# A hybrid retention / state-space block: matmuls of the state-space parts tied behind the projections and spread over v, phase powers and uT laid out contiguously, the query decay moved into the group norm

## The chip, the core and the metric

The kernel runs on one core of a Trainium2 chip. The metric is the time of one execution on the device in microseconds; lower is better. Three runs of the kernel before are shown, and one further execution, the profiled one, left the trace that every row below comes from.

## What is computed

One decoder block in float32: x has 1024 positions of 1024 channels. `w_in` gives q, k, v, gate (512 channels each) and u (512). Four retention heads of 128 work on q, k, v; 32 groups of 16 channels of u go through a diagonal state-space model with 64 complex states each; the two results go through `w_out`, and a squared-ReLU MLP with 4096 hidden channels follows. What matters here, cut from the reference:

```python
h = rmsnorm(x, norm_mix_pre[i]);  proj = h @ w_in[i]
q, k, v, gate, u = jnp.split(proj, [512, 1024, 1536, 2048], axis=-1)
...
s = jnp.einsum('bnihk,bnjhk->bnhij', q, k) * decay          # chunks of 128 positions
inner = jnp.einsum('bnhij,bnjhd->bnihd', s, v)
xi = jnp.exp((idx + 1.0)[None, :] * log_gamma[:, None])     # decay of a query's row
cross = jnp.einsum('bnihk,bnhkd,hi->bnihd', q, R_prev, xi)
y_ret = head_groupnorm(inner + cross)                       # (y - mean) * rsqrt(var + 1e-6) * g
...
states = associative_scan(a2 * a1, a2 * x1 + x2)            # over positions, complex
y_ssm = gelu(real(states @ c) + d_skip * u);  a, b = split(y_ssm @ w_glu[i])
x = x + rmsnorm(concat([y_ret, a * sigmoid(b)]) @ w_out[i], norm_mix_post[i])
m = square(relu(rmsnorm(x, norm_mlp_pre[i]) @ w_ff1[i])) @ w_ff2[i]
x = x + rmsnorm(m, norm_mlp_post[i])
```

## The kernel before

Large products keep float32 accuracy with three passes: ScalarE (ACT) rounds an operand to its high part `hi_*` (L135, L138), VectorE (DVE) subtracts to get the low part `lo_*` (L136), and `mm3` issues three matmuls of 128x512 (L106: hi·hi, hi·lo, lo·hi). Activations lie channels by positions, in two halves of 512 positions (`hf`), so most tiles are 128x512. A scheduler orders each engine's instructions when the program is built, and `tc.add_manual_dep` adds order where the code wants it: `mm` notes every large matmul in `marks`, `load` puts a DMA on SyncE's queue (SP, L115) not earlier than a mark some us back, and SP's queue issues in order, so a DMA that waits holds up those behind it.

The stages in time order, with the stretch each has in the profile:

- u projection (to 52 us): four tiles a half. ACT copies each from PSUM to `us` (L276) and the broadcast norm factor to `R` (L282). DVE multiplies them into `uT` (L285), writing 8 interleaved positions apart (`p t n`, with 64 x 8 read the other way), and SP writes uT to DRAM (`ud`), from where eight DMAs a part gather `UT` (positions by 8 times 16 channels on the partitions).
- small tables for the state-space model, on DVE, then the phase powers `fa` (16 powers) and `fb` (16 powers of the 16th), by repeated complex products on GpSimd (POOL, `double_up`, L312 to L317 with engine `GP`): one chain of 50 small instructions. A complex product takes six instructions (`cmul`).
- gate projections `pg` of the four heads, then q and k projections `pj` of heads 0 and 1, then `v_all`, then q and k of heads 2 and 3. Each half of a projection is 24 large matmuls, and so is each of v's 8 blocks. Between them the generator `side` runs the state-space parts in 24 steps: `tick()` advances it by one in each half of a gate, q or k projection, `v_all` in every second of its blocks. So 16 steps fall ahead of v, 4 into v, and 4 into the projections of heads 2 and 3.
- `ssm_part(ei)`, eight parts of four groups: `phase_tables` for every second part (L312 to L317 with engine `V`: `Fr`, `Fi` from `fa` and `fb`, 128x512), `W` and `VV` (outer products, three DVE instructions each, L493 to L495), `kps` (L502), `MR` (a memset by GpSimd at L506 and eight DMAs), `wps`, then `xps` (L522) from `UT`, the products with the phases on DVE (L523 to L526), the scan (L529), `SS` (L539), `MT` on ACT (L541), and `yps` (L544, L545), whose second matmul of each group needs `SS`. Gelu and a DMA to `yd` end a part.
- retention per head and half (`head_half`): `st`, masked by `dm`; `kz`, the states `Rs`; q is multiplied by `xis` (L630) and meets `Rs` in `y` (L638); group norm, and a transposition into the gate's tile.
- GLU (`gl`), W_out (`mx`), the norms, and the MLP from about 450 us to the end, which the change leaves as it is.

TensorE (PE) takes its instructions in order: a state-space matmul that is not ready holds up the projections behind it.

Of the kernel before, what the change touches and what calls it, by code (L numbers as in the profile page):

```python
# [18 lines left out]
AF = mybir.ActivationFunctionType  # L19
# [5 lines left out]
P = 128  # L25
# [3 lines left out]
T = 8  # L29
# [21 lines left out]
def hybrid_block_kernel(ctx, tc, x, xrow, gain, wu, wv, wqkg, wglu, wout, wff1, wff2, lam, bc, dsk,  # L51
# [116 lines left out]
    gains = const("gains", [P, 36])  # L168
    load(gains, gain)
    g_pre, g_post = gains[:, 0:8], gains[:, 8:16]  # L170
# [48 lines left out]
    def rstd(name, sums, n):  # L219
# [4 lines left out]
        return r  # L224

    def in_place(gen):

        n, last[0] = len(marks), None
        next(gen, None)
        stat[0] = last[0]  # L230
        if stat[0] is not None:
            tc.add_manual_dep(stat[0].ins, marks[n - 1][1].name, gate_info, reason="in order")
# [34 lines left out]
    for hf in range(2):  # L267
        n64 = slice(hf * 64, hf * 64 + 64)
        pss = [acc_ps(f"u_{hf}_{b}") for b in range(4)]
        for k in range(KB):  # L270
            for b in range(4):
                mm3(pss[b], tuple(z[:, b * P:(b + 1) * P] for z in wus[k]), hT[k][hf],
                    k == 0, k == KB - 1)
        us = [half(f"us_{hf}{b}") for b in range(4)]
        for b in range(4):
            S.activation(us[b], pss[b], AF.Copy)  # L276
        sums = xsum[:, 0, 4 * hf:4 * hf + 4]
        V.tensor_tensor(sums, sums, xsum[:, 1, 4 * hf:4 * hf + 4], op=ADD)
        rr = rstd(f"x{hf}", sums, 4)
        rv.append(rr)  # L280
        R.append(half(f"R{hf}"))
        S.activation(R[hf], norm_bcast(f"x{hf}", rr, 4), AF.Copy)  # L282
        for b in range(4):
            uT = half(f"uT_{hf}{b}", shape=(P, T, 64))
            V.tensor_tensor(uT.rearrange("p t n -> p n t"), us[b].rearrange("p (n t) -> p n t", t=T),  # L285
                            R[hf].rearrange("p (n t) -> p n t", t=T), op=MUL)
            load(ud[:, b * P:(b + 1) * P, n64].rearrange("t c n -> c t n"), uT)
# [123 lines left out]
    G2 = G // 2  # L411
    fa = half("fa", shape=(P, 2, 16, G2))
    fa_r, fa_i = fa[:, 0], fa[:, 1]
    fb = half("fb", shape=(P, 2, T, G))[:, :, :, 0:G2]
# [35 lines left out]
    def phase_tables(j):  # L450

        gs = slice(4 * j, 4 * j + 4)
        shf = [P, 4, T, 16]

        def lowp(m):
            return m[:, :, gs].rearrange("p a g -> p g a").unsqueeze(2).to_broadcast(shf)

        def highp(m):
            return m[:, :, gs].rearrange("p a g -> p g a").unsqueeze(3).to_broadcast(shf)

        def v4(m):
            return m.rearrange("p g (b a) -> p g b a", a=16)

        even, odd = ([half(f"F{z}{2 * j + i}", shape=s3) for z in "ri"] for i in range(2))
        tr, ti = half(f"ftr{j}", shape=s3), half(f"fti{j}", shape=s3)
        cmul(V, V, v4(even[0]), v4(even[1]), lowp(fa_r), lowp(fa_i), highp(fbr), highp(fbi),
             v4(tr), v4(ti))
        for e, o in zip(even, odd):
            load(o[0:64], e[64:128])
            load(o[64:128], e[64:128])  # L470
            load(e[64:128], e[0:64])
        phases[2 * j], phases[2 * j + 1] = even, odd

    def ssm_part(ei):
# [26 lines left out]
        for g in range(4):  # L501
            TE.matmul(kps[:, g], W[:, g], cs[:, g0 + g], start=True, stop=True)  # L502
        S.activation(kt, kps, AF.Copy)
# [17 lines left out]
        for g in range(4):  # L521
            TE.matmul(xps[:, g], WT[:, g], UT[:, g], start=True, stop=True)  # L522
        V.tensor_tensor(A, xps, Fr, op=MUL)  # L523
# [19 lines left out]
        for g in range(4):  # L543
            TE.matmul(yps[:, g], MT[:, g], UT[:, g], start=True, stop=False)  # L544
            TE.matmul(yps[:, g], VV[:, g], SS[:, g], start=False, stop=True)  # L545
# [15 lines left out]
    def step(n=1):  # L561
        for _ in range(n):
            next(side, None)
# [4 lines left out]
    def v_all():  # L568
# [3 lines left out]
        for c in range(NCH):  # L572
            if c % 2 == 0:
                step(1)
            ps = acc_ps(f"v_{c}")
# [8 lines left out]
    for i in range(2):  # L584
# [6 lines left out]
        tabs.append(pair)  # L591
    dm, xis = half("dm", shape=(P, H, P)), half("xis", shape=(P, H, P))
    load(dm, dmask, 10.0)
    load(xis, xi, 10.0)
    zet = const("zet", [P, H])
# [10 lines left out]
    def head_half(h, hh, qh, kh, sgt, Rs, gam):  # L606
# [16 lines left out]
        for i in range(n_s):  # L623
# [3 lines left out]
            else:  # L627
                V.scalar_tensor_tensor(Rs[c // 4][:, c % 4], Rs[(c - 1) // 4][:, (c - 1) % 4], gam,
                                       sps[:, i], op0=MUL, op1=ADD)
        V.tensor_tensor(q_, q_, xis[:, h].unsqueeze(1).to_broadcast(list(s3)), op=MUL)  # L630
        yield
# [10 lines left out]
        rs, nmr = ring("rs", (P, 4), 3), ring("nmr", (P, 4), 3)  # L642
        V.tensor_scalar(rs, mv[:, :, 1], EPS, None, op0=ADD)
        GP.tensor_tensor(rs, rs, mhalf[:, 0:4], op=ALU.pow)
# [527 lines left out]
def _constants():  # L1172
# [11 lines left out]
    dmask = np.where(diff[:, None, :] >= 0,  # L1184
                     np.exp(np.maximum(diff, 0.0)[:, None, :] * lg[None, :, None]), 0.0) * scale
    xi = np.broadcast_to(np.exp((loc + 1.0)[None, None, :] * lg[None, :, None]), (P, H, P))
    zeta = np.exp((P - 1 - loc)[:, None] * lg[None, :]) * scale
# [71 lines left out]
```

## Time and profile before

| quantity | value |
|---|---|
| runs | 1079.92, 1077.33, 1080.24 us (median 1079.92) |
| profiled execution, its own time | 1078.81 us |
| span of its trace | 1076.0 us |
| TensorE | 1048.2 us busy, 97% |
| VectorE / ScalarE / GpSimd | 72% / 46% / 7% busy |

The span is from the first to the last instruction; the 2.8 us beside it lie around the program. A row of a timeline has the start in us, the duration, engine, line, operation, output and inputs, shape, and, in brackets, how long the engine had been idle before it and what released it. PE's instructions overlap, so its rows last longer (0.39 us) than the distance of their starts (0.227 us for a 128x512 matmul); a lost time is read from the starts. A float32 matmul of a state-space part stands as two records.

### The profile page before, as it was taken

To read this page: it belongs to the slowest core of one execution; us is meant where nothing else is said; L and a number is where in the kernel's file an instruction comes from. 1 tells how busy PE (TensorE), PEld (TensorE's weight loads), DVE (VectorE), ACT (ScalarE), POOL (GpSimd) and SP (SyncE) were. 2 spreads that over 40 slices of the span, in tenths; PEclk is the share of its full clock that TensorE was granted. 3 is DMA by queue.
4 is the path that set the end of the run, shared out by engine and by line. 5 is a ranking of instruction groups with operands and counts; after the bars stand their busy time and mean duration, and the time that the engine had idled before them with its cause. 6 is when DMAs were issued, how large, how long until landed. Compare 5 with 4: busy or idle time off the path is not lost.

```text
span 1076.0 us, 14905 instructions
## 1 busy us (share of the span) xinstructions
PE 1048.2 (97%) x5056; PEld 879.4 (82%) x5056; DVE 769.5 (72%) x1446; ACT 490.9 (46%) x916; POOL 74.1 (7%) x101
## 2 busy tenths in 40 slices
PE   7999999999999999999999999999999999999995
PEld 6878778888888788788888888888888888888895
DVE  7979998278775207478888888877763885765965
ACT  7512343154564324466644444564731553524712
POOL 0360000000100222300000000000000000000002
PEclk9999999999999999999999999999999999999998
DMA  9735342042421105396366666656972665569424
GB/s 327 255 77 137 92 128 82 19 118 74 140 72 40 40 1 196 116 314 226 126 226 233 235 232 231 210 185 212 376 276 75 190 210 165 180 218 340 137 84 152
DMA packets 126283, 181.55 MB, mean 169 GB/s; under 512 B 35584, under 2 KB 43776, under 8 KB 126208
## 3 DMA queue, kind: packets, MB, share of 16 engines
q1 hardware_dynamic: 125664, 180.09, 50.5%
q8 instruction: 39, 0.64, 0.2%
q10 hardware_dynamic: 544, 0.52, 0.1%
q14 instruction: 36, 0.29, 0.1%
HBM read 130.62 MB, written 45.61 MB: 164 GB/s over the span
## 4 chain that ended last, share of the span: by engine, by line
PE 79%; DVE 6%; DMA 3%; POOL 2%; issue 2%; ACT 2%; SPq 1%; DVEq 0%; ACTq 0%; POOLq 0%
PE f2x L106 15%; PE f2y L106 12%; PE f1z L106 8%; PE f1y L106 8%; PE mx L106 8%; PE f1x L106 8%; PE pj L106 5%; PE v L106 4%; PE f1w L106 4%; PE gl L106 3%; SPq L115 1%; DMA yd<-Y 1%; PE sps L622 1%; DMA raw_wglu<-wglu_dram 1%; PE y L636 0%
## 5 line engine op out<-in xcount | busy, mean ns | idle before, releaser
L106 PE MATMUL f2x<-hi_tc,lo_sb 128*128 128x512 f32 x216 | 84.0, 389 | 0.0
L106 PE MATMUL f2x<-lo_tc,hi_sb 128*128 128x512 f32 x216 | 84.0, 389 | 0.0
L106 PE MATMUL f2x<-hi_tc,hi_sb 128*128 128x512 f32 x216 | 83.7, 390 | 0.0
L135 ACT ACTIVATE hi_sa<-rawa 128x512 fp32r<-128x512 f32 x80 | 48.4, 623 | 60.3 <-DVE rawa L828 57.1
L106 PE MATMUL f2y<-hi_tc,hi_sb 128*128 128x512 f32 x192 | 74.7, 389 | 0.0
L106 PE MATMUL f2y<-lo_tc,hi_sb 128*128 128x512 f32 x192 | 74.7, 389 | 0.0
L106 PE MATMUL f2y<-hi_tc,lo_sb 128*128 128x512 f32 x192 | 74.7, 389 | 0.0
L136 DVE TENSOR_TENSOR lo_sa<-rawa,hi_sa 128x512 fp32r<-128x512 f32 x80 | 56.5, 712 | 10.3 <-ACT hi_sa L135 10.3
L223 POOL TENSOR_TENSOR small<-small 128x4 f32<-128x4 f32 (+1 forms) x9 | 11.7, 1303 | 658.6 <-DVE small L221 628.1
L106 PE MATMUL pj<-hi_h,hi_wqkg 128*128 128x512 f32 x128 | 51.1, 399 | 0.0
L106 PE MATMUL pj<-hi_h,lo_wqkg 128*128 128x512 f32 x128 | 50.3, 393 | 0.0
L106 PE MATMUL pj<-lo_h,hi_wqkg 128*128 128x512 f32 x128 | 50.3, 393 | 0.0
L106 PE MATMUL f1x<-lo_tb,hi_sa 128*128 128x512 f32 x128 | 49.9, 390 | 0.3 <-DVE lo_tb L136 0.3
L106 PE MATMUL f1x<-hi_tb,hi_sa 128*128 128x512 f32 x128 | 50.1, 392 | 0.0
L106 PE MATMUL f1y<-hi_tb,hi_sa 128*128 128x512 f32 x128 | 49.8, 389 | 0.0
L106 PE MATMUL f1y<-lo_tb,hi_sa 128*128 128x512 f32 x128 | 49.8, 389 | 0.0
L106 PE MATMUL f1y<-hi_tb,lo_sa 128*128 128x512 f32 x128 | 49.8, 389 | 0.0
L106 PE MATMUL f1z<-hi_tb,hi_sa 128*128 128x512 f32 x128 | 49.8, 389 | 0.0
L106 PE MATMUL f1z<-lo_tb,hi_sa 128*128 128x512 f32 x128 | 49.8, 389 | 0.0
L106 PE MATMUL f1z<-hi_tb,lo_sa 128*128 128x512 f32 x128 | 49.8, 389 | 0.0
L106 PE MATMUL f1x<-hi_tb,lo_sa 128*128 128x512 f32 x128 | 49.3, 390 | 0.0
L106 PEld LDWEIGHTS f2x<-lo_tc,hi_sb 128*128 128x128 f32 x216 | 40.6, 188 | 8.4
(398 smaller groups left out, 2929.6 us busy)
## 6 DMA issues: line engine op xcount, KB each, us to landing
rawa<-wff_dram SPq DMA_DIRECT2D x92, 256.0 KB, 3.2
tinx<-td SPq DMA_DIRECT2D x48, 256.0 KB, 4.0
tiny<-td SPq DMA_DIRECT2D x48, 256.0 KB, 3.6
raw_wqkg<-wqkg_dram SPq DMA_DIRECT2D x24, 256.0 KB, 3.1
x<-x_dram SPq DMA_DIRECT2D x16, 256.0 KB, 5.4
xt<-xrow_dram SPq DMA_DIRECT2D x16, 256.0 KB, 5.4
raw_wo<-wout_dram SPq DMA_DIRECT2D x16, 256.0 KB, 3.7
xr<-x_dram SPq DMA_DIRECT2D x16, 256.0 KB, 3.3
```

What stands on the lines that cost most here:

```text
L106: r = TE.matmul(out_, lhsT, rhs, **kw)
L115: r = nc.sync.dma_start(dst, src)
L135: after_mark(S.activation(hi, src, AF.Copy))
L136: V.tensor_tensor(lo, src, hi.bitcast(F32), op=SUB)
L223: GP.tensor_tensor(r, t, mhalf[:, 0:n], op=ALU.pow)
L622: TE.matmul(sps[:, i], kz[:, i], v_[:, i], start=True, stop=True)
```

## The change

Six edits:

1. The gains (128x36) are loaded by ACT's own DMA queue rather than as the first entry of SP's.
2. `not_before`: the first matmul of each `kps`, `xps` and `yps` is ordered not earlier than the last large matmul written before it in the program.
3. ACT writes `us` already permuted (eight writes of 64 x 8 with a stride) and a second, permuted copy of the norm factor, `Rt` (two instructions more). `uT` becomes a plain product of contiguous tiles.
4. `fa` is laid out with its 16 powers innermost; GpSimd's chain over the powers then steps 64 bytes from element to element, and DVE's phase products read `fa` contiguously.
5. `v_all` advances the state-space generator in each of its 8 blocks rather than in every second, so that the last step falls into v.
6. q is no longer multiplied by the query decay. The group norm removes a row's factor up to its epsilon, so a table of epsilons per row and head takes its place, and the mask's table carries the inverse factor. One 256 KB load and eight DVE products go.

```diff
...
     gains = const("gains", [P, 36])
-    load(gains, gain)
+    S.dma_start(gains, gain)
     g_pre, g_post = gains[:, 0:8], gains[:, 8:16]
...
+    def not_before(r):
+        tc.add_manual_dep(r.ins, marks[-1][1].name, gate_info, reason="no earlier")
...
                     k == 0, k == KB - 1)
-        us = [half(f"us_{hf}{b}") for b in range(4)]
+        us = [half(f"us_{hf}{b}", shape=(P, T, 64)) for b in range(4)]
         for b in range(4):
-            S.activation(us[b], pss[b], AF.Copy)
+            S.activation(us[b].rearrange("p t n -> p n t"), pss[b].rearrange("p (n t) -> p n t", t=T), AF.Copy)
         sums = xsum[:, 0, 4 * hf:4 * hf + 4]
...
         R.append(half(f"R{hf}"))
-        S.activation(R[hf], norm_bcast(f"x{hf}", rr, 4), AF.Copy)
+        nb = norm_bcast(f"x{hf}", rr, 4)
+        Rt = half(f"Rt{hf}", shape=(P, T, 64))
+        S.activation(Rt.rearrange("p t n -> p n t"), nb.rearrange("p (n t) -> p n t", t=T), AF.Copy)
+        S.activation(R[hf], nb, AF.Copy)
         for b in range(4):
             uT = half(f"uT_{hf}{b}", shape=(P, T, 64))
-            V.tensor_tensor(uT.rearrange("p t n -> p n t"), us[b].rearrange("p (n t) -> p n t", t=T),
-                            R[hf].rearrange("p (n t) -> p n t", t=T), op=MUL)
+            V.tensor_tensor(uT, us[b], Rt, op=MUL)
             load(ud[:, b * P:(b + 1) * P, n64].rearrange("t c n -> c t n"), uT)
...
     G2 = G // 2
-    fa = half("fa", shape=(P, 2, 16, G2))
-    fa_r, fa_i = fa[:, 0], fa[:, 1]
+    fa = half("fa", shape=(P, 2, G2, 16))
+    fa_r, fa_i = (fa[:, i].rearrange("p g a -> p a g") for i in range(2))
     fb = half("fb", shape=(P, 2, T, G))[:, :, :, 0:G2]
...
         def lowp(m):
-            return m[:, :, gs].rearrange("p a g -> p g a").unsqueeze(2).to_broadcast(shf)
+            return fa[:, m, gs].unsqueeze(2).to_broadcast(shf)
...
         tr, ti = half(f"ftr{j}", shape=s3), half(f"fti{j}", shape=s3)
-        cmul(V, V, v4(even[0]), v4(even[1]), lowp(fa_r), lowp(fa_i), highp(fbr), highp(fbi),
+        cmul(V, V, v4(even[0]), v4(even[1]), lowp(0), lowp(1), highp(fbr), highp(fbi),
              v4(tr), v4(ti))
...
         for g in range(4):
-            TE.matmul(kps[:, g], W[:, g], cs[:, g0 + g], start=True, stop=True)
+            r = TE.matmul(kps[:, g], W[:, g], cs[:, g0 + g], start=True, stop=True)
+            if g == 0:
+                not_before(r)
         S.activation(kt, kps, AF.Copy)
...
         for g in range(4):
-            TE.matmul(xps[:, g], WT[:, g], UT[:, g], start=True, stop=True)
+            r = TE.matmul(xps[:, g], WT[:, g], UT[:, g], start=True, stop=True)
+            if g == 0:
+                not_before(r)
         V.tensor_tensor(A, xps, Fr, op=MUL)
...
         for g in range(4):
-            TE.matmul(yps[:, g], MT[:, g], UT[:, g], start=True, stop=False)
+            r = TE.matmul(yps[:, g], MT[:, g], UT[:, g], start=True, stop=False)
+            if g == 0:
+                not_before(r)
             TE.matmul(yps[:, g], VV[:, g], SS[:, g], start=False, stop=True)
...
         for c in range(NCH):
-            if c % 2 == 0:
-                step(1)
+            step(1)
             ps = acc_ps(f"v_{c}")
...
         tabs.append(pair)
-    dm, xis = half("dm", shape=(P, H, P)), half("xis", shape=(P, H, P))
+    dm = half("dm", shape=(P, H, P))
     load(dm, dmask, 10.0)
-    load(xis, xi, 10.0)
+    epsx = const("epsx", [P, H])
+    load(epsx, xi)
     zet = const("zet", [P, H])
...
                                        sps[:, i], op0=MUL, op1=ADD)
-        V.tensor_tensor(q_, q_, xis[:, h].unsqueeze(1).to_broadcast(list(s3)), op=MUL)
         yield
...
         rs, nmr = ring("rs", (P, 4), 3), ring("nmr", (P, 4), 3)
-        V.tensor_scalar(rs, mv[:, :, 1], EPS, None, op0=ADD)
+        V.tensor_scalar(rs, mv[:, :, 1], epsx[:, h:h + 1], None, op0=ADD)
         GP.tensor_tensor(rs, rs, mhalf[:, 0:4], op=ALU.pow)
...
     dmask = np.where(diff[:, None, :] >= 0,
-                     np.exp(np.maximum(diff, 0.0)[:, None, :] * lg[None, :, None]), 0.0) * scale
-    xi = np.broadcast_to(np.exp((loc + 1.0)[None, None, :] * lg[None, :, None]), (P, H, P))
+                     np.exp(-(loc + 1.0)[:, None, None] * lg[None, :, None]), 0.0) * scale
+    xi = EPS * np.exp(-2.0 * (loc + 1.0)[:, None] * lg[None, :])
     zeta = np.exp((P - 1 - loc)[:, None] * lg[None, :]) * scale
...
```

Instruction order, first SP's queue at the loads of part 0's `UT0` and the write of `uT_11` (second block of uT, second half of the positions) to DRAM. Before:

```order
L115 DMA MR1_888<-small_72 128x64
L115 DMA UT0_794<-ud_284 16x4x128 x6
L115 DMA ud_284<-uT_11_538 128x8x64
L115 DMA UT0_794<-ud_284 16x4x128 x2
L115 DMA UT1_867<-ud_284 16x4x128 x2
```

After:

```order
L115 DMA MR1_891<-small_72 128x64
L115 DMA UT0_797<-ud_284 16x4x128 x2
L115 DMA ud_284<-uT_11_542 128x8x64
L115 DMA UT0_797<-ud_284 16x4x128 x6
L115 DMA UT1_870<-ud_284 16x4x128 x5
L115 DMA ud_284<-uT_12_545 128x8x64
```

The write of uT_11 stood ahead of the last two loads of UT0 and now stands ahead of the last six.

On DVE, the same uT_11 and the first phase table (`Fr0`, `fti0`, `ftr0`, `Fi0`). Before:

```order
L493 TENSOR_TENSOR W2_1087<-bc0_276,qw_608 128x512
L312 TENSOR_TENSOR Fr0_776<-fa_667,fb_668 128x512
L316 TENSOR_TENSOR fti0_781<-fa_667,fb_668 128x512
L313 TENSOR_TENSOR ftr0_780<-fa_667,fb_668 128x512
L285 TENSOR_TENSOR uT_11_538<-us_11_518,R1_528 128x64x8
L315 TENSOR_TENSOR Fi0_777<-fa_667,fb_668 128x512
L495 TENSOR_TENSOR W2_1087<-W2_1087,tmpw2_1088 128x512
L136 TENSOR_TENSOR lo_wqkg8_0_943<-raw_wqkg8_0_940,hi_wqkg8_0_942 128x512
```

After:

```order
L499 TENSOR_TENSOR W2_1090<-bc0_276,qw_612 128x512
L292 TENSOR_TENSOR uT_11_542<-us_11_520,Rt1_536 128x512
L501 TENSOR_TENSOR W2_1090<-W2_1090,tmpw2_1091 128x512
L500 TENSOR_TENSOR tmpw3_1272<-bc1_277,qw_612 128x512
L136 TENSOR_TENSOR lo_wqkg8_0_946<-raw_wqkg8_0_943,hi_wqkg8_0_945 128x512
L318 TENSOR_TENSOR Fr0_779<-fa_671,fb_672 128x512
L322 TENSOR_TENSOR fti0_784<-fa_671,fb_672 128x512
L319 TENSOR_TENSOR ftr0_783<-fa_671,fb_672 128x512
```

uT_11 and three more (the sum of W2, tmpw3 and one lo part) moved from behind the first phase product to ahead of it.

On POOL, the end of the `fb` chain, which the first phase product waits for, and the memset of `MR2`. Before:

```order
L312 TENSOR_TENSOR fb_668<-fb_668 128x16
L313 TENSOR_TENSOR t8_610<-fb_668 128x16
L315 TENSOR_TENSOR fb_668<-fb_668 128x16
L316 TENSOR_TENSOR t8_610<-fb_668 128x16
L314 TENSOR_TENSOR fb_668<-fb_668,t8_610 128x16
L317 TENSOR_TENSOR fb_668<-fb_668,t8_610 128x16
L506 MEMSET MR2_1099 128x512
```

After:

```order
L514 MEMSET MR2_1102 128x512
L320 TENSOR_TENSOR fb_672<-fb_672,t8_614 128x2x16
L323 TENSOR_TENSOR fb_672<-fb_672,t8_614 128x2x16
L318 TENSOR_TENSOR fb_672<-fb_672 128x16
L319 TENSOR_TENSOR t8_614<-fb_672 128x16
L321 TENSOR_TENSOR fb_672<-fb_672 128x16
L322 TENSOR_TENSOR t8_614<-fb_672 128x16
L320 TENSOR_TENSOR fb_672<-fb_672,t8_614 128x16
L323 TENSOR_TENSOR fb_672<-fb_672,t8_614 128x16
```

The memset moved from behind the chain's last product to eight instructions ahead of its end; it writes the buffer that part 0's MR0 had, so it comes after `MT0` on ACT, MR0's reader.

## Rows read from the trace of the kernel before

**Rows 1.** From the page: each engine's busy time, share of the span and instructions.

```profile
PE 1048.2 (97%) x5056; PEld 879.4 (82%) x5056; DVE 769.5 (72%) x1446; ACT 490.9 (46%) x916; POOL 74.1 (7%) x101
```

**Rows 2.** Waits of PE from 0 to 350 us: total, times, longest, in us.

```profile
PE yps L545 <- DVE SS L539: 5.2, 4, 1.7
PE xps L522 <- DMA UT<-ud: 2.6, 1, 2.6
PE gl L106 <- ACT rb L689: 1.6, 1, 1.6
```

**Rows 3.** Windows: length, busy us of PE, PEld, DVE, ACT, POOL, PEclk, DMA, GB/s.

```profile
54.00:81.00 27.00, 24.36 (x114) 20.30 (x113) 19.39 (x27) 5.14 (x10) 16.08 (x43) 0.94 0.32 76
81.00:108.00 27.00, 25.97 (x139) 21.82 (x138) 26.77 (x46) 7.73 (x13) 0.53 (x1) 1.00 0.51 137
...
200.00:225.00 25.00, 25.00 (x133) 21.34 (x132) 11.22 (x21) 8.45 (x23) 0.00 (x0) 1.00 0.28 82
225.00:250.00 25.00, 25.00 (x146) 21.82 (x145) 18.05 (x32) 10.09 (x15) 0.00 (x0) 1.00 0.24 62
```

**Rows 4.** Timeline of PE around part 0's xps, and at the last late yps.

```profile
73.70 0.39 PE L106 MATMUL pg<-hi_h,lo_wqkg 128*128 128x512 f32 x1
73.92 0.39 PE L106 MATMUL pg<-hi_h,hi_wqkg 128*128 128x512 f32 x1
76.95 1.36 PE L522 MATMUL xps<-UT,WT 128*128 128x128 f32 x8 [2.64 <-DMA UT<-ud]
78.39 0.77 PE L106 MATMUL pg<-lo_h,hi_wqkg 128*128 128x512 f32 x1
...
81.34 0.40 PE L106 MATMUL pg<-hi_h,lo_wqkg 128*128 128x512 f32 x1
...
152.14 0.49 PE L545 MATMUL yps<-SS,VV 128*128 128x128 f32 x2 [1.70 <-DVE SS L539]
```

**Rows 5.** Timeline of SP's queue, part 0's loads.

```profile
64.17 3.26 SPq L115 DMA_DIRECT2D UT<-ud  x6
73.39 0.38 SPq L115 DMA_DIRECT2D ud<-uT  x1
73.81 2.06 SPq L115 DMA_DIRECT2D UT<-ud  x4
```

**Rows 6.** Timeline of DVE: start of the phase products, and part 3's SS.

```profile
63.43 0.67 DVE L493 TENSOR_TENSOR W<-bc,qw 128x512 f32<-128x512 f32 x1
69.41 1.06 DVE L312 TENSOR_TENSOR Fr<-fa,fb 128x512 f32<-128x512 f32 x1 [5.31 <-POOL fb L314]
...
72.27 1.09 DVE L285 TENSOR_TENSOR uT<-us,R 128x512 f32<-128x512 f32 x1
...
150.79 0.69 DVE L136 TENSOR_TENSOR lo_wqkg<-raw_wqkg,hi_wqkg 128x512 fp32r<-128x512 f32 x1 [0.95 <-ACT hi_wqkg L135]
151.40 0.68 DVE L539 TENSOR_TENSOR SS<-A,C 128x508 f32<-128x508 f32 x1
```

**Rows 7.** Timeline of POOL: the power chain and the memset behind it.

```profile
55.20 3.82 POOL L314 TENSOR_TENSOR fa<-fa,t 128x32 f32<-128x32 f32 x1
...
62.97 0.46 POOL L314 TENSOR_TENSOR fa<-fa,t 128x128 f32<-128x128 f32 x1
...
69.34 0.22 POOL L317 TENSOR_TENSOR fb<-fb,t 128x16 f32<-128x16 f32 x1
74.22 0.53 POOL L506 MEMSET MR<- 128x512 f32 x1 [4.66 <-ACT MT L541]
```

**Rows 8.** Timeline of ACT: the first hi part, MT0, and the end of the heads.

```profile
4.98 0.72 ACT L138 ACTIVATE hi_h<-x,small 128x512 fp32r<-128x512 f32 x1 [0.20 <-DMA small<-gain_dram]
...
73.53 0.64 ACT L541 ACTIVATE MT<-MR 128x512 f32<-128x512 f32 x1 [6.43 <-DVE uT L285]
...
288.42 1.12 ACT L135 ACTIVATE hi_s<-ysT 128x512 fp32r<-128x512 f32 x1 [2.06 <-DMA ysT<-yd]
```

**Rows 9.** DVE by form, 225 to 345 us: busy us, mean ns, idle before.

```profile
L630 DVE TENSOR_TENSOR ra<-ra,xis 128x512 f32<-128x512 f32 x8 | 5.5, 685 | 0.0
```

## Prediction

> **What bounds the kernel now.** I read the page first: TensorE is busy 97% of the span, every other engine well below [rows 1]. So the kernel gains only where PE loses time, and the second view is the list of what PE waits for. Between the start and 350 us it has three entries that the change touches: `yps` waiting for DVE's `SS`, four times and 5.2 us; part 0's `xps` waiting for its loads `UT`, 2.6 us; and `gl` waiting for an eviction by ACT, 1.6 us [rows 2]. From 450 us on nothing is touched.
>
> Then each wait by its own stretch. Part 0's `xps` issues at 76.95, three us after the matmul before it, and the matmuls behind it are slow for a while: 78.39 to 81.34 holds seven, 0.42 us each against 0.22 us from 73.70 to 73.92 [rows 4]. [...] The wait goes back over SP: the last loads of UT0 issue at 73.81 behind the write of uT_11 at 73.39 [rows 5], which waited for DVE's uT_11 at 72.27; that stood behind three phase products, and the first of these began at 69.41, when POOL's power chain was done [rows 6, 7].
>
> From there DVE is full: 26.77 of 27 us in the window from 81 to 108 [rows 3]. The four late `yps` follow DVE's order, the last one being SS of part 3 at 151.40 and its matmul at 152.14, 0.74 us later [rows 4, 6]. So from 69.4 to 152 us DVE sets the time, behind POOL.
>
> **The change part by part.**
>
> *uT and its place.* uT_11 now stands ahead of the phase products and its inputs come from ACT and PE, so its write no longer waits for POOL. Six UT loads took SP 3.26 us from 64.17; the last loads before had landed 3.1 us after 73.81 [rows 4, 5]. Two loads, the write and six loads from 64.2 should be in by about 70. xps0 stands six matmuls earlier in PE's order, 73.9 - 6 x 0.22 = 72.6: the whole stall goes, with some 2.5 us to spare. What goes is the wait, 76.95 - 73.92 - 0.22 = 2.8 us, and the slow matmuls, 7 x (0.42 - 0.22) = 1.4 us. **4.2 us.** The moved writes pass nothing on SP that waits longer.
>
> *DVE from the first phase product to SS of part 3.* Before this took 151.40 - 69.41 = 82.0 us. In it lie 14 phase products of 1.05 us [rows 6]. The new layout has 16 contiguous elements beside a broadcast one, which is the form of `W`, 0.67 us [rows 6]: 14 x 0.37 = 5.2 us (bounds 0 and 5.2; I take 5.0). Two uT there become contiguous, 2 x 0.4 = 0.8. Four instructions move ahead of the first product, into DVE's idle 5.31 us: uT_11 about 1.0 and three of 0.6, 2.8. The idle 0.95 us ahead of SS3 [rows 6] has no reason once the rest is earlier. One more lo part comes in, 0.6 against. 82.0 - 5.0 - 0.8 - 2.8 - 0.9 + 0.6 = 73.1 us. With T for the start of the first phase product, SS3's matmul can go at T + 73.1 + 0.7 = T + 73.8. PE itself would be there at 152.14 - 4.2 - 5.2 = 142.7. With T = 69.4, as before, the four waits together would be 0.5 us rather than 5.2.
>
> *T, the end of POOL's chain.* Two things lengthen it. MR2's memset, 0.53 us, now stands inside it [rows 7]. And POOL's instructions are held up while DVE runs: one of 32 elements took 3.82 us, where one of 128 elements takes 0.46 [rows 7]; four DVE instructions more now run beside the chain, about 2.6 us in their new, shorter form. So T lies between 69.9 and 72.6. Of the chain's other rows none is near 3.82 us, so I take a small part of it, T = 70.3. [...] Then the four yps wait 70.3 + 73.8 - 142.7 = 1.4 us in total. **5.2 - 1.4 = 3.8 us.** One us on T is one us on PE.
>
> [...]
>
> *v and the order of the parts.* `v_all` takes eight steps rather than four, so the last part ends in v. DVE has room there, 11.22 of 25 us in the window from 200 to 225 [rows 3], and the second half of two parts comes into its 8 x 24 matmuls of 0.22 us, 43 us: some 16 DVE instructions a part at about 0.6 us, 19 us (an estimate). Cost 0 while that holds. At the end of the heads, `hi_s` of the last part stood in ACT's queue at 288.42 after waiting 2.06 us for its load [rows 8], and the evictions that `gl` waited for stood behind it [rows 2]. In the new order it comes well ahead of them. **1.6 us** (bounds 0 and 2.6, with the small waits around `mx`).
>
> *The query decay.* Eight DVE products of 685 ns go, 5.5 us, and none was waited for [rows 9]; PE was busy 25.00 of 25 us where they begin, DVE 18.05 [rows 3]. Cover: PE's own work. 0. The epsilon table is one operand in place of another, 0; the mask's constants are other numbers. One load of 256 KB less on SP, 0.
>
> *The gains on ACT's queue.* The first hi part waited 0.20 us for them [rows 8]. **0.2 us** (bounds -0.3 and 0.7).
>
> *ACT's permuted writes.* MT, also permuted, takes 0.64 us; a strided read takes 1.12 [rows 8]. Ten instructions, eight of them replacing plain ones: up to 5 us of ACT, about half in each half of u. ACT idled 6.43 us ahead of MT0 [rows 8], so this is covered; without that, R and uT_1x come up to 2.5 us later, about what UT0 has to spare.
>
> *not_before* only orders; the new order has part 0's kps, xps and yps within some matmuls of where they were. 0.
>
> Sum: 4.2 + 3.8 + 1.6 + 0.2 = 9.8 us. The profiled execution took 1078.8 us, 1.1 below the median of the runs and inside their spread; 1078.8 - 9.8 = **1069.0 us**.
>
> **The rivals.** *The power chain comes late.* The four DVE instructions, the memset and the strided access all land on POOL, and T is 72.6 to 77. For it: the 3.82 us row. Against: most of the chain ran at 0.22 to 0.46 us each. Time 1069.0 + (2.3 to 6.7) = 1071.3 to 1075.7. [...]
>
> *The phase products stay at 1.05 us*, so that the change doesn't do what it says, because the broadcast operand and not `fa` made them slow. 5.0 us return: 1074.0. Against: `W` with its broadcast at 0.67.
>
> *ACT is late.* Permuted evictions of 1.12 us or more bring uT_10 and uT_11 past what SP has to spare; the xps0 stall stays in part, 2 to 4.2 us: 1071 to 1073. *v becomes DVE's*: a yps of parts 5 to 7 waits there as parts 0 to 3 did; 2 to 5 us: 1071 to 1074.
>
> *Slower: the memset stops the chain.* POOL runs in order, and MR2's memset waits for MT0 on ACT, which ran at 73.53 before, held by uT [rows 8]. In the new order MT0 waits for MR0's loads alone and can run near 63. If something still holds it, T is MT0 + 0.6 + 0.5 + 8 x 0.2 = MT0 + 2.7: at 73.5 this is T = 76.2 and 1074.9; it decides against the change from MT0 at about 81, and if MT0 waited for a load that itself waits for the phase table, at 85 say, T = 87.7 and the time is 1086.4.
>
> **How the numbers follow.** Forecast, 0.58: 1069.0, with T from 69.4 to 72.6 and the 1.6 and 0.2 at their bounds, 1066.5 to 1072. Chain late 0.17, products long 0.06, ACT late 0.06, v late 0.05, memset 0.04; 0.04 is left for what no row points to, either way. A measurement of this kernel tells 0.3% from no change, 3.2 us: below 1076.7 of the median is faster. All cases but the memset at its worst and the upper end of a chain made late are below it: faster 0.88, within 0.08, slower 0.04. The range of 8 in 10 reaches into the late chain and the long products: 1065.5 to 1075.
>
> **What would show it.** After the change: no wait of xps on UT and a granted clock of 1.00 from 54 to 81 us; the first phase product at 70 to 71, phase products of about 0.68 us, uT likewise; yps waits of 1 to 2 us in all; no wait of gl on rb; POOL's instructions on fa at most 0.1 us longer. I am wrong if POOL's last fb product ends after 73, if MT0 comes after 70, or if yps waits appear in v.

## The result

The kernel after takes 1070.76 us in the median of four runs (1069.04 to 1071.44), the kernel before 1080.08 us (four runs, 1077.33 to 1081.0): a ratio of 0.9915, 95% interval 0.9894 to 0.9937. That is 9.3 us less; 9.8 were forecast. The profiled executions, 1078.81 before and 1069.04 after, lie 9.8 us apart; that this is the forecast to a tenth is chance, as the profiled execution after is the fastest of its four. The sum came out, but three of its four terms did not, and that their errors cancelled was luck.

The page of the kernel after, TensorE's waits up to 350 us (total, times, longest, in us), and the window in which its clock had been 0.94:

```profile
PE 1044.9 (98%) x5056; PEld 878.9 (82%) x5056; DVE 758.7 (71%) x1438; ACT 494.8 (46%) x918; POOL 72.4 (7%) x101
```

```profile
PE u L106 <- ACT hi_wu L135: 6.4, 1, 6.4
PE yps L557 <- DVE SS L549: 2.8, 3, 1.5
```

```profile
54.00:81.00 27.00, 27.00 (x141) 22.94 (x140) 20.29 (x32) 7.60 (x13) 17.77 (x41) 1.00 0.33 80
```

Against [rows 2] the waits of xps and gl are gone, that of yps has fallen from 5.2 to 2.8 us, and PE is busy throughout the window that had 24.36 of 27 us [rows 3]. The first matmul, at 5.75 us before, comes at 6.40. Reading PE's lost time from the starts of its matmuls, with the slow matmuls behind a wait counted in, the parts are:

| place | lost before | lost after | gained | forecast |
|---|---|---|---|---|
| xps of part 0, itself slow, and the slow matmuls after it | 4.4 | 0 | 4.4 | 4.2 |
| yps of parts 0 to 3 | 5.8 | 3.6 | 2.2 | 3.8 |
| gl on rb, and the small waits at gl and mx | 3.1 | 0 | 3.1 | 1.6 |
| first matmul | 5.75 | 6.40 | -0.65 | 0.2 |

These are some 9.1 of the 9.4 us by which the span fell; the rest is in spacings too small to name.

How xps became free: the loads on SP and the rows of DVE around the first phase product, after.

```profile
63.82 1.00 SPq L115 DMA_DIRECT2D UT<-ud  x2
64.92 0.38 SPq L115 DMA_DIRECT2D ud<-uT  x1
65.35 5.33 SPq L115 DMA_DIRECT2D UT<-ud  x11
```

```profile
63.68 0.67 DVE L292 TENSOR_TENSOR uT<-us,Rt 128x512 f32<-128x512 f32 x1
...
71.62 0.69 DVE L318 TENSOR_TENSOR Fr<-fa,fb 128x512 f32<-128x512 f32 x1 [5.11 <-POOL fb L320]
...
83.96 0.69 DVE L533 TENSOR_TENSOR A<-xps,Fr 128x512 f32<-128x512 f32 x1 [0.81 <-DMA Fr<-Fr]
...
146.05 0.68 DVE L549 TENSOR_TENSOR SS<-A,C 128x508 f32<-128x508 f32 x1
```

uT_11 runs at 63.68 and its write goes out at 64.92, where [rows 5] had 73.39; all loads of UT0 are issued by 69. The phase products take 0.68 us where [rows 6] had 1.06. But the first of them starts at 71.62, not at the 70.3 of the sum, still behind an idle 5.11 us. POOL's rows tell where the chain lost the time:

```profile
55.59 2.74 POOL L320 TENSOR_TENSOR fa<-fa,t 128x64 f32<-128x64 f32 x1
...
60.91 0.64 POOL L321 TENSOR_TENSOR fa<-fa 128x128 f32<-128x128 f32 x1
...
63.03 2.32 POOL L323 TENSOR_TENSOR fa<-fa,t 128x128 f32<-128x128 f32 x1
65.31 0.72 POOL L439 TENSOR_SCALAR fb<-fa 128x16 f32<-128x16 f32 x1
66.00 0.64 POOL L440 TENSOR_SCALAR fb<-fa 128x16 f32<-128x16 f32 x1
...
69.75 0.52 POOL L514 MEMSET MR<- 128x512 f32 x1
```

The memset inside the chain took 0.52 us, as forecast, and did not wait: MT0 ran at 64.07 on ACT, where [rows 8] had 73.53. The instructions up to L440 ended 1.8 us later than before. Some of them are longer because `fa` is strided, others took longer while DVE worked beside them; the section on the prediction takes the two apart.

The start is the term with the wrong sign. In the trace of the kernel before, the gains were the third load on SP's queue and not the first, and ACT loaded the table for its activations at once:

```profile
0.74 1.28 ACT L135 ACT_TABLE_LOAD   x1 [0.74 <-PEq L1249]
```

The first rows of ACT, its queue among them, and of PE, after:

```profile
0.73 0.40 ACTq L169 DMA_DIRECT2D small<-gain_dram  x1
3.81 1.28 ACT L138 ACT_TABLE_LOAD   x1 [3.81 <-DMA x<-x_dram]
5.11 0.72 ACT L138 ACTIVATE hi_h<-x,small 128x512 fp32r<-128x512 f32 x1
```

```profile
6.40 2.07 PE L106 MATMUL u<-hi_h,hi_wu 128*128 128x512 f32 x4 [6.40 <-ACT hi_wu L135]
```

ACT's table load takes 1.28 us. It stands right ahead of the first activation and here waits for x, which that activation needs. The gains are no longer waited for; the table load has taken their place.

### The profile page after: what moved, and what is told of

It reads as the page before. It is cut to its first block, busy times and chain, and to the rows that moved or that the text cites. A ratio compares the mean times of both kernels' runs of the same rounds, so it can differ in the third digit from the quotient of the medians.

```text
span 1066.6 us, 14890 instructions
## 1 busy us (share of the span) xinstructions
PE 1044.9 (98%) x5056; PEld 878.9 (82%) x5056; DVE 758.7 (71%) x1438; ACT 494.8 (46%) x918; POOL 72.4 (7%) x101
## 4 chain that ended last, share of the span: by engine, by line
PE 85%; DVE 4%; POOL 2%; issue 2%; DMA 1%; SPq 1%; ACT 0%; DVEq 0%; POOLq 0%; ACTq 0%
PE f2x L106 16%; PE f2y L106 12%; PE f1z L106 8%; PE f1y L106 8%; PE mx L106 8%; PE f1x L106 8%; PE pj L106 7%; PE v L106 4%; PE gl L106 4%; PE f1w L106 4%; SPq L115 1%; PE y L649 1%; PE st L625 1%; PE yps L557 1%; PE y L651 1%
## 5 line engine op out<-in xcount | busy, mean ns | idle before, releaser
L106 PEld LDWEIGHTS f2x<-hi_tc,hi_sb 128*128 128x128 f32 x216 | 40.6, 188 | 8.5 <-issue 0.3
```

The costliest lines, as they stand in the source:

```text
L106: r = TE.matmul(out_, lhsT, rhs, **kw)
```

## The experiments

All are versions of the kernel before or after. Times are medians, of four runs where no number is given. Ratios, with their 95% intervals, are to the kernel before on the same chip; they are worked out from all runs and are not quite the quotient of the medians. Where the intervals of two versions overlap, the distance of their medians is not clear of noise.

**One edit undone at a time: the gains back on SP's queue.**

```diff
-    S.dma_start(gains, gain)
+    load(gains, gain)
```

> The kernel after with one edit undone: the gains are again the third load on SP's queue. In the kernel after PE's first matmul comes at 6.40 us, before at 5.75, and ACT's table load at 3.81 rather than 0.74. Theory (the table load, standing behind ACT's own DMA issue, takes over the wait of the first activation for x): the table load returns to 0.7 us, the first matmul to 5.7 to 5.8, the time is 0.6 us below the kernel after, the rest of the trace as after. Rival (the first matmul is late because hi_h now stands ahead of hi_wu, or the loads of x land later by chance): the first matmul stays at 6.3 to 6.4 and the time within 0.1 us of after by the place of the first matmul.

Measured: 1070.49 us, ratio 0.9922 (0.9895 to 0.9949), the same as after. ACT's table load, the first yps, PE's waits, and the window behind that yps:

```profile
0.73 1.28 ACT L135 ACT_TABLE_LOAD   x1 [0.73 <-PEq L1262]
```

```profile
96.67 0.49 PE L557 MATMUL yps<-SS,VV 128*128 128x128 f32 x2 [2.58 <-DVE SS L549]
```

```profile
PE u L106 <- ACT hi_h L138: 5.9, 1, 5.9
PE yps L557 <- DVE SS L549: 3.4, 2, 2.6
```

```profile
97.00:101.00 4.00, 4.00 (x19) 3.54 (x18) 3.94 (x7) 0.00 (x0) 0.00 (x0) 0.59 0.34 72
```

The table load is back at 0.73 and the first matmul at 5.9, half a us earlier than after. The theory on the start holds. The time does not follow, since PE only arrives earlier at the first yps, which DVE has ready no sooner, and the longer wait (2.58 us for 1.47) is followed by matmuls at a granted clock of 0.59. Time won ahead of a wait that another engine sets is not won.

**uT back on DVE, with plain evictions by ACT.**

```diff
...
-            S.activation(us[b].rearrange("p t n -> p n t"), pss[b].rearrange("p (n t) -> p n t", t=T), AF.Copy)
+            S.activation(us[b], pss[b], AF.Copy)
...
-            V.tensor_tensor(uT, us[b], Rt, op=MUL)
+            V.tensor_tensor(uT.rearrange("p t n -> p n t"), us[b].rearrange("p (n t) -> p n t", t=T),
+                            R[hf].rearrange("p (n t) -> p n t", t=T), op=MUL)
```

> The kernel after with one edit undone: ACT copies us plain, no Rt, uT on DVE with strided reads and writes. uT_11 still stands ahead of the first phase product in DVE's order. Theory (xps0's stall went because of the place of uT_11, not because of who permutes): no wait of xps on UT; POOL's chain ends 0.5 to 1.5 us earlier or later as DVE's longer uT (1.08 for 0.68 us) hold it, two uT of 0.4 us more inside DVE's full stretch, yps waits 2.5 to 4.5 us against 2.8, time within 0 to 2 us of the kernel after. Rival (the permuting by ACT is what brings uT forward): the wait of xps on UT is back at 1.5 to 2.6 us with slow matmuls behind it, time 3 to 4.5 us above after.

Measured: 1070.46 us, 0.9923 (0.9895 to 0.9952), the same as after: no wait of xps, yps 3.0 us. Who permutes is worth nothing here. uT_11 still runs ahead of the first phase product (65.82 and 72.29 us), as the theory had it.

**The same, and fa laid out as before.**

```diff
-    fa = half("fa", shape=(P, 2, G2, 16))
-    fa_r, fa_i = (fa[:, i].rearrange("p g a -> p a g") for i in range(2))
+    fa = half("fa", shape=(P, 2, 16, G2))
+    fa_r, fa_i = fa[:, 0], fa[:, 1]
...
-            return fa[:, m, gs].unsqueeze(2).to_broadcast(shf)
+            return fa[:, m, :, gs].rearrange("p a g -> p g a").unsqueeze(2).to_broadcast(shf)
```

> The kernel after with two edits undone: uT as above, and fa laid out as before (powers not innermost). In this order uT_11 stands behind the first phase product again and its write behind seven loads of UT0. Against the run with uT alone undone this is the worth of the layout of fa. Theory: phase products 1.05 us for 0.68, 14 of them before the fourth SS, so yps waits 4 to 5 us more than there; POOL's fa instructions of 128 elements at 0.45 rather than 0.65 or more and the first phase product 1 to 1.5 us earlier; xps waits on UT again for 2 to 3 us; in all 5 to 8 us above the run with uT alone undone. Rival (the layout is worth little, the gain of the change is in not_before and the spread over v): within 2 us of it.

Measured: 1079.12 us (ten runs, 1078.10 to 1079.95), 0.9999 (0.9987 to 1.0012): 8.7 us above the run with uT alone undone, and no gain left over the kernel before. PE's waits, the rows of DVE behind them, and those of SP ahead of xps:

```profile
PE pg L106 <- DVE ga L685: 8.3, 1, 8.3
PE u L106 <- ACT hi_wu L135: 6.7, 1, 6.7
PE xps L529 <- DMA Fr<-Fr: 1.3, 1, 1.3
```

```profile
69.77 1.04 DVE L317 TENSOR_TENSOR Fr<-fa,fb 128x512 f32<-128x512 f32 x1 [3.89 <-POOL fb L319]
...
97.22 1.28 DVE L685 TENSOR_TENSOR ga<-pg,R 128x512 f32<-128x512 f32 x2
```

```profile
75.29 0.38 SPq L115 DMA_DIRECT2D ud<-uT  x1
75.71 0.58 SPq L115 DMA_DIRECT2D UT<-ud  x1
```

The first phase product is 1.9 us earlier than after, and each takes 1.04 us again. The loss shows at another place than the theory had it: in this order the products and their followers stand ahead of DVE's eviction of a gate projection, `ga` at 97.22, and PE waits 8.3 us for it. I take it for the same shortage, DVE full from 70 us on, and the place for a matter of the order; the run doesn't part the dearer products from an order that happens to be worse.

The xps of part 0 waits again, 1.3 us where 2 to 3 were expected, and no slow matmuls follow. The profile names a copy of Fr, but xps reads `UT` and `WT`. The last load of UT0 went out at 75.71, behind the write of uT_11, and xps began 2.8 us later, at 78.48; in the kernel before it began 3.1 us after the last two [rows 4, 5]. So I put this wait down to that load. uT_11 runs at 74.18 here, behind the first phase product, as it does in the two other kernels with the old fa (72.27 behind 69.41 in the kernel before [rows 6], 71.78 behind 69.87 in the one with the query decay alone, below). In every version with the new fa it runs ahead. It is the new fa that brings uT_11 forward.

**uT and fa alone, on the kernel before.** No not_before, gains on SP, v and the query decay as before. fa alone was not run.

> The kernel before with two edits done: fa with its powers innermost, and uT permuted by ACT. The gains on SP's queue, no not_before, v as before, the query decay's products in place. Theory (the layout of fa gives most of the gain, since undoing it with uT cost 8.7 us where undoing uT alone cost nothing): phase products 0.68 us, first phase product near 72, xps without a wait, yps waits 3 to 4 us; 6 to 8.5 us below before. Rival (fa helps only together with not_before and the spread): 0 to 3 us below before.

Measured: 1070.76 us (1069.45 to 1071.42), 0.992 (0.9901 to 0.994): 9.4 us below before, more than the theory had, and all of the gain.

```profile
PE yps L557 <- DVE SS L549: 2.9, 4, 1.7
PE gl L106 <- ACT rb L703: 1.7, 1, 1.7
```

The yps waits are those of the kernel after, and xps has none. The gl wait of 1.7 us is there, so its going belongs to the other edits. They win it, and lose 0.9 us at the start (6.40 us after, 5.49 here); what is left of that is smaller than the spread of the runs.

**v with a step in every second block, as before.**

```diff
         for c in range(NCH):
-            step(1)
+            if c % 2 == 0:
+                step(1)
```

> The kernel after with one edit undone: v_all advances the state-space parts in every second block only, so the last four steps fall into the projections of heads 2 and 3 as before. Up to v nothing differs: first phase product at 71.6, yps waits 2.8 us, no wait of xps on UT. Theory (the 1.6 us wait of gl on rb and the 1.3 us of small gaps at gl and mx went with the spread): they return, 1.5 to 3.1 us, time 1.5 to 3 us above after. Rival (they went with the query decay's products, or with other reordering at the heads): no such waits, time within 0.5 us of after.

Measured: 1069.82 us (1069.23 to 1069.98), 0.9914 (0.9891 to 0.9938). No wait of gl or mx comes back. The theory fell, and with it the reason that the prediction gave for the 1.6 us.

**The query decay multiplied again,** in the kernel after (`xis` loaded, eight products, the old mask and epsilon):

> The kernel after with one edit undone: q is multiplied by the query decay again (eight DVE products of 0.69 us, one load of 256 KB) and the group norm has its plain epsilon. Undoing the spread over v brought no wait of gl back, so what removed the 1.6 us wait of gl on rb (3.1 us with the small gaps at gl and mx) is open. Theory (it went with these products, which moved the work at the end of the heads): waits of gl or mx of 1.5 to 3 us are back, time 1.5 to 3 us above after. Rival (it went because everything ahead of it comes 7 us earlier, or with the spread and this one doing the same): no such waits, time within 0.5 us of after.

Measured: 1073.42 us (six runs, 1069.97 to 1075.63), 0.9946 (0.9928 to 0.9965), some 2.7 us above after, though the intervals overlap. Theory and rival both miss: the time is up, but nothing waits at gl. The profiled execution is the slowest of the six; its waits are these:

```profile
PE yps L557 <- DVE SS L549: 6.2, 5, 2.1
PE xps L530 <- DMA UT<-ud: 0.5, 1, 0.5
```

In this order the first phase product starts at 72.78, 1.2 us later than after, and the yps wait 6.2 us; what in the order does it was not traced.

**The query decay alone, on the kernel before:**

> The kernel before with one edit done alone: the query decay left to the group norm. All else as before: the xps wait of 2.6, the yps waits of 5.2, the start at 5.75. Theory (the gl wait hangs on this edit): no wait of gl on rb, the small gaps at mx gone too, time 1.5 to 3 us below before. Rival (the gain is in the order ahead of it): the gl wait of 1.6 us stays, time within 0.5 us of before.

Measured: 1076.93 us (ten runs), 0.9976 (0.9959 to 0.9993), 3.2 us below before. The gl and mx waits are gone, those of xps and yps stand:

```profile
PE yps L556 <- DVE SS L548: 5.2, 3, 2.5
PE xps L529 <- DMA UT<-ud: 2.6, 1, 2.6
```

So the gl wait goes when the query decay's products go, with nothing else done. In the run before this one the products were back, and it stayed away. That run differs from uT and fa alone, which has the wait, by the spread over v, not_before and the gains; that the spread keeps it away there is likely and not shown.

**No not_before** (the function does nothing):

> The kernel after with one edit undone: no ordering of kps, xps and yps behind the last large matmul. The order on DVE and POOL hardly differs, on PE a few state-space matmuls stand some places earlier. Theory (this edit is worth nothing by itself here): first phase product near 71.6, yps waits 2.5 to 3.5 us, time within 0.7 us of after. Rival (it keeps PE from standing in front of matmuls that are not ready): yps or kps waits grow by 1 to 3 us and the time with them.

Measured: 1070.70 us, 0.9911 (0.9894 to 0.9928), yps waits 2.4 us: worth nothing.

**What sets the yps waits.** Two versions of the kernel after, both with the gains on SP's queue. First the memsets from MR2 on ordered behind the last product of fb (`fb_end`):

```diff
...
-        GP.memset(MR, 0.0)
+        behind(GP.memset(MR, 0.0), fb_end if ei >= 2 else None)
```

> The kernel after with the gains on SP's queue and MR2's memset ordered behind the last fb product, so that 0.52 us leave POOL's chain. To be held against the run with the gains on SP's queue, where the first phase product is at 71.96, yps waits are 3.4 us and five matmuls behind the first of them are slow. Theory (one us on the end of POOL's chain is one us on PE): first phase product 0.5 us earlier, yps waits 0.5 us less, 0.5 us gained, up to 1.6 us if the gap ahead of the first yps gets short enough that the slow matmuls go as well. Rival (DVE's own load sets the yps): waits as there, time within 0.2 us.

Measured: 1068.11 us (1067.67 to 1068.51), 0.9888 (0.9873 to 0.9903). Against the run with the gains undone the first phase product is 1.0 us earlier, twice the memset's time:

```profile
70.93 0.69 DVE L318 TENSOR_TENSOR Fr<-fa,fb 128x512 f32<-128x512 f32 x1 [4.66 <-POOL fb L320]
```

The yps wait 2.8 us instead of 3.4, and no slow matmuls follow the first. With these (1.1 us) PE loses 1.6 us less there; 2.4 us came off the median, but the intervals of the two ratios touch. The part on the chain holds by sign, the size is above what the waits explain.

Then the fb chain moved from POOL to DVE, with two raw buffers (for weights as they are loaded) in place of three, for room in SBUF:

```diff
...
-    GP.tensor_scalar(fbr[:, 1], fa_r[:, 15], 1.0, None, op0=MUL)
-    GP.tensor_scalar(fbi[:, 1], fa_i[:, 15], 1.0, None, op0=MUL)
+    V.tensor_scalar(fbr[:, 1], fa_r[:, 15], 1.0, None, op0=MUL)
+    V.tensor_scalar(fbi[:, 1], fa_i[:, 15], 1.0, None, op0=MUL)
     for w, n in ((1, 1), (2, 2), (4, 2)):
-        double_up(fbr[:, 1:], fbi[:, 1:], 1, w, n, GP)
-    double_up(fbr[:, 1:], fbi[:, 1:], 1, 6, 1, GP)
+        double_up(fbr[:, 1:], fbi[:, 1:], 1, w, n)
+    double_up(fbr[:, 1:], fbi[:, 1:], 1, 6, 1)
```

> The kernel after with the chain of fb (26 small instructions) on DVE instead of POOL, the gains on SP's queue, and two raw buffers rather than three for the projections' weights, so that it fits. In the kernel after DVE waits 5.1 us for POOL's fb; POOL takes 0.21 to 0.25 us for each and the memset 0.52, DVE takes 0.10 to 0.20 for an instruction of this size. Theory (the end of the chain, T = 71.6, sets the yps waits, one us for one us): the chain ends 1 to 3 us earlier, yps waits fall from 2.8 by as much to 0 to 2 us, no slow matmuls behind them, the start at 5.8 now counts as well (0.6): time 1.5 to 4 us below after. Rival (DVE's own load sets the yps, not T): the same yps waits though T is earlier, time within 0.7 us of after. Against it: the two raw buffers could hold up loads of weights, seen as waits of PE on lo or hi parts.

Measured: **1065.27 us** (1064.64 to 1066.19), 0.9872 (0.9853 to 0.989), 5.5 us below the kernel after and the fastest of all. PE waits for nothing between its first matmul and the MLP, for weights neither. The two buffers without the fb chain on DVE were not run, so their share of this is not shown. What DVE waits for between 50 and 155 us, the kernel after first, then this one:

```profile
DVE Fr L318 <- POOL fb L320: 5.1, 1, 5.1
DVE small L512 <- POOL t L319: 2.9, 1, 2.9
DVE A L533 <- DMA Fr<-Fr: 0.8, 1, 0.8
```

```profile
DVE small L512 <- ACT small L511: 3.1, 1, 3.1
DVE fb L439 <- POOL fa L320: 2.1, 1, 2.1
```

Three rows of DVE there, and two of POOL's last doubling, at which DVE stood idle (from 60.6 to 62.6):

```profile
62.64 0.47 DVE L439 TENSOR_SCALAR fb<-fa 128x16 f32<-128x16 f32 x1 [2.07 <-POOL fa L320]
63.15 0.17 DVE L318 TENSOR_TENSOR fb<-fb 128x16 f32<-128x16 f32 x1
...
71.69 0.67 DVE L318 TENSOR_TENSOR Fr<-fa,fb 128x512 f32<-128x512 f32 x1
```

```profile
60.91 0.63 POOL L321 TENSOR_TENSOR fa<-fa 128x128 f32<-128x128 f32 x1
...
62.09 0.52 POOL L320 TENSOR_TENSOR fa<-fa,t 128x128 f32<-128x128 f32 x1
```

The theory was that T, the start of the first phase product, sets the yps. T is 71.69 here, as after, and yet the waits are gone: DVE spent the 5.1 us on other work instead of waiting, with fb in between at about 0.1 us from one start to the next (63.93, 64.01, 64.09, 64.18), and had less left behind T. The rival of the expectation, that T matters little, was half right. My reading is that DVE's idle time ahead of SS counts, of which the wait for POOL was the largest piece. It rests on these two traces and is not the whole: with uT and fa alone DVE waits only 1.7 us for POOL's fb, and the yps wait 2.9 us all the same. Over the versions with the new fa the yps waits don't follow T: 2.9 us at T = 70.76 (uT and fa alone), 2.1 at 72.26 (v as before), 6.2 at 72.78 (the query decay multiplied again).

Last, the same with the gains on ACT's queue and a small activation ahead of it, so that the table load waits for nothing:

```diff
...
+    warm = const("warm", [P, 2])
+    V.memset(warm, 0.0)
+    S.activation(warm, warm, AF.Copy)
     S.dma_start(gains, gain)
```

> The kernel with the fb chain on DVE (1065.27 us), but with the gains on ACT's queue again, and a two-element activation of a constant ahead of their issue, so that ACT's table load has nothing to wait for. Theory (the late first matmul of the kernel after comes from the table load that waits for x): table load in the first 2 us, first matmul at 5.2 to 5.8 instead of 6.4, and since no later wait takes it up, a time 0 to 0.5 us below 1065.27. Rival (a first activation on ACT's queue is late for the queue's own sake): first matmul at 6.2 or later, time 0.5 to 0.8 us above 1065.27.

Measured: 1069.73 us (1067.35 to 1071.43), 0.9899 (0.9875 to 0.9923), 4.5 us above the version without by the medians, with intervals that overlap a little. The start did what the theory said, and other waits came in:

```profile
1.17 1.28 ACT L171 ACT_TABLE_LOAD   x1 [1.17 <-PEq L1265]
4.09 0.72 ACT L138 ACTIVATE hi_h<-x,small 128x512 fp32r<-128x512 f32 x1 [1.43 <-DMA small<-gain_dram]
```

```profile
PE u L106 <- ACT hi_wu L135: 5.4, 1, 5.4
PE yps L560 <- DVE SS L552: 1.1, 2, 0.7
PE v L106 <- DVE lo_wva L136: 0.7, 1, 0.7
PE v L106 <- DVE lo_wvb L136: 0.4, 1, 0.4
```

The first matmul is at 5.38, the earliest of all. The order behind it changed with the instruction more and the gains on the other queue, and yps and the lo parts of v wait for DVE again. Read from the starts of its matmuls PE loses 3.4 us in these places and at one kps, of 4.5 us between the medians; the rest stays open. So two small instructions at the start can take back most of what the fb chain on DVE had won, and the 5.5 us are those of one order.

## Why the prediction was right, and where not

*xps.* Right in mechanism, and nearly in size: 4.2 forecast, 4.4 found, with the clock back at 1.00. The 0.2 are xps's own matmuls, which ran slow as well: 1.44 us from its start to the next large matmul, 1.03 after. The cause named, the place of uT_11, holds. What puts it there is the new fa and not ACT's permuting: DVE's strided uT leaves it ahead, the old fa puts it behind.

*DVE's full stretch.* The phase products came to 0.68 us, the step that carried the gain, and the rival that they stay at 1.05 is out. The stretch from T to the fourth SS is 146.05 - 71.62 = 74.4 us, not 73.1: 0.8 of the difference is DVE's wait for the copies of Fr (the row at 83.96), which the sum did not have; the other 0.5 was not traced.

*T.* 71.62 for 70.3, the term that was mis-sized, though it lay inside its stated ends of 69.9 to 72.6. The memset counted as forecast. The strided accesses to fa, for which the sum had nothing, counted too: with no DVE beside them, instructions of 128 elements took 0.63 and 0.52 us for 0.46 [rows 7]. An estimate from all such rows of the kernel after and of the runs with the gains undone and the fb chain on DVE (128 elements 0.52 to 0.64 us for 0.45, 64 elements 0.28 to 0.41 for 0.31, 16 and 32 elements at most 0.05 more) is 1.0 us for the 24 instructions on fa, most of the 1.3 by which T was late.

Instructions with DVE beside them took 2.7, 2.3 and, on fb, 0.7 and 0.6 us; the kernel before has such rows too (3.82 [rows 7] and 1.04 at 63.39), so this is mostly not new. Beside the two longest, from 55.59 to 58.33 and from 63.03 to 65.35, DVE ran four products and sums of 128x512 each (55.63 to 58.10 and 63.08 to 65.90), beside the 3.82 us in the kernel before five (55.24 to 59.02). What in them makes POOL's instruction last so long was not shown.

*yps.* 2.2 us for 3.8, by the later T and the longer stretch. "One us on T is one us on PE" held by sign where only the memset left the chain. It is no rule: the fb chain on DVE left T at 71.69 and no wait at all.

*gl.* The wait went, with 1.5 us of small waits besides, 3.1 us in all where the upper bound was 2.6, but the reason was wrong: not the spread over v alone. The query decay, put at 0 because its products lay under PE's work, is enough to remove it. The step that failed is "none was waited for, so it costs nothing": the products cost nothing as work, but taking them out changes the order of the heads.

*The start.* -0.65 for 0.2, outside its bounds of -0.3 to 0.7. The prediction looked at what the first activation waited for, and not at the table load in front of it, which had begun at 0.74 in the kernel before.

*v, not_before, ACT's writes.* As forecast, nothing. ACT's permuted writes did take about 1.1 us, the upper end, and were covered.

*The signs.* Three that were named did not come: the first phase product at 70 to 71 (71.62), yps waits of 1 to 2 us (2.8), and instructions on fa at most 0.1 us longer (up to 0.19). None of those that were to prove the forecast wrong came either.

So the layout of fa carried the forecast and the result: with uT it gives all of the gain, and without the two nothing is left. uT alone undone costs nothing.

## What to carry to other kernels

When an engine is full over a stretch, a cheaper form of its commonest instruction is worth its count times the saving, here 14 x 0.37 = 5.2 of the 7.6 us by which the stretch shrank. Price it from the stretch and not from one wait, since the saving can show at any instruction that waits for this engine. An engine that idles in front of a full stretch is a good place to look next: with the small chain that DVE had waited for on DVE itself, at some 0.1 us an instruction beside GpSimd's 0.2, the time was 5.5 us lower, though one raw buffer fewer was part of that run and an order slightly changed took 4.5 back. Where a scheduler sets the order, a small edit can move waits elsewhere by as much as it saves, so one edit's price is known only from runs with and without it.

## What had not been expected of the hardware

- With a DMA issue first on ACT's queue the table load (1.28 us) came at 3.81 instead of 0.73 us, behind the wait for x; an activation of two elements ahead of the issue brought it to 1.17. In the late case hi_h, which reads x, is also the first activation, in the early one hi_wu; which of the two counts was not separated.
- ACT's eviction with a permuted write took 1.11 us in the mean where the plain one took 0.59, after and before:

```profile
L280 ACT ACTIVATE us<-u 128x512 f32<-128x512 f32 x8 | 8.3, 1114 | 7.2 <-PE u L106 7.2
L276 ACT ACTIVATE us<-u 128x512 f32<-128x512 f32 x8 | 4.7, 594 | 4.5 <-PE u L106 4.4
```

- The granted clock fell after some waits of PE and not after others: matmuls ran slow (0.59 from 97 to 101 us) behind 2.58 us of waiting in the run with the gains undone, and at full speed (1.00) behind the 1.47 us of the kernel after. The length of the wait alone doesn't tell: in the run with v as before the clock was 0.67 from 97 to 101 us, behind 1.90 us of waiting ahead of 97.08, while in the run with the query decay alone PE waited 2.6 us ahead of xps and the clock of 54 to 81 us was 1.00, where the kernel before shows 0.94 with a wait of 2.64 [rows 3, 4].
